# Hybrid attention and linear-attention layer on one core: values and gates loaded behind queries and keys, first sums of the last rows loaded early, first half of the out-projection spread over 20 steps more

## The chip, the cores and the metric

One core of a Trainium2 chip runs the kernel. The metric is the device time of one execution in microseconds. Three timed runs of the kernel before gave 996.18, 999.50 and 999.75 us (median 999.50); the profiled execution took 1000.02 us.

## The reference, cut to what matters

```python
h = rms_norm(x, pre_g)                       # x: 1024 rows of 1024
z = h @ w_in                                 # all projections at once
qa, ka, va, ga, qb, kb, vb, gb, gk_low = split_columns(z)
...
for each of 8 heads, 2 maps m, causal:       # differential attention, head size 2 x 64
    p[m] = softmax(mask(q[m] @ k[m].T * 64**-0.5))
    oa = (p[0] - lam * p[1]) @ v             # v: 1024 x 128
oa = rms_norm(oa, subln_g) * 0.8 * silu(ga)
...
ob = rms_norm(gla_chunked(qb, kb, vb, log_a), gla_g) * silu(gb)   # 4 heads, linear attention
y = concat([oa, ob]) @ w_out                 # 2048 -> 1024
return x + rms_norm(y, post_g)
```

All operands are float32. The kernel splits each operand of a product into a high and a low part (`hi`, `lo`) and forms the product from three matmuls (hi by hi, lo by hi, hi by lo).

## The kernel before, in words

**Three stages.** Until about 634 us the core computes the projections (accumulators `x`, `y`, `z` in the rows of the profile) and, woven in, the linear attention. Their results go to DRAM: queries and keys per head (`qk_d`), values (`v_d`), gates (`g_d`), and the linear attention's mixed output (`mixe`). Then follows the attention with the out-projection, and last the finishing of the eight blocks of 128 output rows.

**The attention stage is woven from three streams** by `merge`. Each stream is a generator that yields the cost of what it has just issued; a stream has a begin and an end on a common scale of steps and a total cost, and the one that is furthest behind issues next. The streams are:

- `all_scores`: head after head, row blocks qb from 7 down to 0. PE forms the scores (`sc`, first from `k`, then from `ks`, the other split of the keys), DVE takes the row maximum with the mask (L1037), ACT the exponential (L1047), POOL and DVE combine the two maps (L1053, L1056). After block 4 of a head the next head's queries and keys are loaded by `load_qk` (L877, L880) as far as their memory allows.
- `all_values`: PE turns the probabilities (`wtr`), ACT and DVE split them (`wt_hi`, `wt_lo`), PE multiplies by the values (`po`). Each head has a half 1 (rows 512 to 1023) that comes first and a half 0. `load_v` (L988) loads the next head's values after half 1; `attn_norm` loads the gate (L1118), forms the mean square with a matmul of ones (`ms`), applies norm and gate on POOL (L1140) and stores the result to DRAM (`mixd`, L1141). Of head 7 the result stays in memory as `last_mix`.
- `out_early`: the out-projection, as far as its inputs exist. First the linear attention's eight slices for all row blocks `st` (384 matmuls, `ypart`), then the slices of heads 0 to 3 (192 more `ypart`, stored from tile `yst` by a POOL DMA that adds to DRAM, L1304). These sums, `yd`, are read back at the end (tile `yp`) and copied by ACT into PSUM (`seed`, L1365), where PE adds the slices of heads 4 to 7 (`yps`). For the first blocks in the order `ENDS` = 4, 5, 6, 7, 0, 1, 2, 3, this begins inside the stage: slices of heads 4 to 6 are reloaded from `mixd` by `mix_pair` (tile `m_raw`, L1210), and slice 7 comes from `last_mix` (`last_part`, L1229).

**What sets the order.** PE's matmuls run in the order in which the source writes them; the other engines' and the DMA queue's order is chosen by a scheduler while the program is built. `tc.issue_after(ins)` puts what is issued inside it behind `ins` on the same queue; it is an order and no wait for the transfer. All loads and most stores go through the queue of SP, which issues one after the other: an instruction whose memory is not free yet holds all behind it.

**Memory.** Pools `kp` and `sm` hold tiles by tag. `kp` has one buffer each of 4 KB per partition for `q0`, `q1`, `k0`, `k1`, `ks0`, `ks1`. Odd heads put the first half of their keys (`k0`, `ks0`) into `sm` instead, so that `kp`'s `k0` and `ks0` are read for the last time by head 6, and `q0` by head 7. `yst` has two buffers of 2 KB; before the change both the sums that go out (`yst`) and the sums that come back within the stage (`yp`, L1312, L1323, L1338) share them.

Of the kernel before, what the change touches and what calls it, by code (L numbers as in the profile page):

```python
# [8 lines left out]
F32 = mybir.dt.float32  # L9
# [5 lines left out]
P = 128  # L15
# [16 lines left out]
def hymba_kernel(  # L32
# [58 lines left out]
    v_d = [tc.dram_tile([2, P, NT, P], F32, name=f"v{h}_d") for h in range(DA_HEADS)]  # L91
    g_d = [tc.dram_tile([P, S], F32, name=f"g{h}_d") for h in range(DA_HEADS)]
# [7 lines left out]
    yd = [[tc.dram_tile([P, 512], F32, name=f"y{st}{dh}_d") for dh in range(2)] for st in range(NT)]  # L100
# [3 lines left out]
    def bank(i, shape, name):  # L104
        return psum.tile(shape, F32, tag=f"b{i}", name=name)
# [47 lines left out]
    kp = ctx.enter_context(tc.tile_pool(name="kp", bufs=1))  # L153
# [63 lines left out]
    i = order.index((1, 4))  # L217
# [650 lines left out]
    def load_qk(h, n, half):  # L868

        if h % 2 and half == 0 and n != "q":  # L870
            t = smps[0].tile([P, 2, 512], F32R, tag=f"{n}0", name=f"{n}0")
        else:
            t = kp.tile([P, 2, 512], F32R, tag=f"{n}{half}", name=f"{n}{half}")
        for m in range(2):
            d = qk_d["q" if n == "q" else "k"][h][m, :, :, cols(half)]
            if n != "ks":
                sp.dma_start(fp(t[:, m]), d.rearrange("t p s -> (t p) s"))  # L877
            else:
                for i in range(2):
                    sp.dma_start(fp(t[64 * i : 64 * i + 64, m]), d[1 - i])  # L880
        qk[h, n, half] = t

    qk, smps = {}, []


    go(order.index((12, 5)) - made[0])
# [61 lines left out]
    SC, TR, PO, Y = order_b[:3], order_b[3:5], order_b[5], order_b[6:]  # L948
# [22 lines left out]
    smp = smp_cm.__enter__()  # L971
# [13 lines left out]
    def load_v(h):  # L985
        v = [smp.tile([P, NT, P], F32R, tag="v", name=f"v{t}", bufs=4) for t in range(2)]
        for t in range(2):
            ins = sp.dma_start(fp(v[t]), v_d[h][t])  # L988
            if h == 0:
                tc.keep_in_program_order(ins)  # L990
        return v
# [121 lines left out]
    def attn_norm(h, half, o):  # L1113
        if h < DA_HEADS - 1:
            gate = smp.tile([P, 512], F32, tag="gate", name="gate", bufs=2)
        else:
            gate = kp.tile([P, 512], F32, tag=("q1", "k1")[half], name="gate")
        sp.dma_start(gate, g_d[h][:, cols(half)])  # L1118
        sq = smp.tile([P, 512], F32, tag="r", name="sq", bufs=1)
        act.activation(sq, o, AF.Square)  # L1120
        hl = smp.tile([P, 2, 512], F32R, tag="sq_hl", name="sq_hl", bufs=1)
        act.copy(hl[:, 0], sq)
        dve.tensor_tensor(hl[:, 1], sq, fp(hl[:, 0]), ALU.subtract)
        if h == DA_HEADS - 1:

            dve.scalar_tensor_tensor(gate, o, sub_g, gate, ALU.mult, ALU.mult)
        yield 0.0
        yield 0.0
        n_tr[0] += 1
        ms = bank(TR[n_tr[0] % 2], [P, 512], "ms")  # L1130
        for i in range(2):
            mm(ms, ones, hl[:, i], start=(i == 0), stop=(i == 1))
        if h == DA_HEADS - 1 and not half:
            opened[TR[n_tr[0] % 2]] = None
        r = smp.tile([P, 512], F32, tag="r", name="r", bufs=1)
        act.activation(r, ms, AF.Ln, bias=eps_t, scale=1.0 / P)
        act.activation(r, r, AF.Exp, scale=-0.5)
        if h < DA_HEADS - 1:
            dve.scalar_tensor_tensor(r, o, sub_g, r, ALU.mult, ALU.mult)
            pool.tensor_tensor(gate, r, gate, ALU.mult)  # L1140
            sp.dma_start(mixd[h * P : (h + 1) * P, cols(half)], gate)  # L1141
            stored.append(h)
        else:
            dve.tensor_tensor(gate, gate, r, ALU.mult)
            last_mix[half] = gate
        yield 0.0
# [102 lines left out]
    def out_early():  # L1249

        part = mix0
        ps = [y_bank(0, dh, "ypart") for dh in range(2)]
        for e in range(E, E + 8):
            yield 1.0
            if e == E:
                nxt = mix(1)
            for dh in range(2):
                times(ps[dh], part, E, dh, e, E + 7)
            yield 1.0
        for dh in range(2):  # L1260
            sp.dma_start(yd[0][dh], y_tile(ps[dh]))
        for st in range(1, NT - 1):
            part, nxt = nxt, mix(st + 1)
            rows = slice(ENDS[st - 1] * P, ENDS[st - 1] * P + P)
            sp.dma_start(out[0, rows, :], x[0, rows, :])
            for dh in range(2):
                ps = y_bank(st, dh, "ypart")
                for e in range(E, E + 8):
                    times(ps, part, E, dh, e, E + 7)
                    yield 0.69  # L1270
                sp.dma_start(yd[st][dh], y_tile(ps))

# [12 lines left out]
        for dh in range(2):  # L1285
            kept = sp.dma_start(yd[NT - 1][dh], y_tile(ps[dh]))
        for n, st in enumerate(ENDS):
            part = nxt
            if n == 1:
                yield lambda: len(stored) >= 8  # L1290
            if n + 3 < NT:
                raws_o.append(load_mix(ENDS[n + 3], 0, 4))

            if 1 <= n <= 4:
                with tc.issue_after(kept.ins), tc.issue_after(mix_load[0]):
                    weights(3 + n)
            if n + 1 < NT:
                nxt = mix_part(ENDS[n + 1], 0, 4, raws_o.pop(0))
            for dh in range(2):
                ps = y_bank(st, dh, "ypart")  # L1300
                for e in range(4):
                    times(ps, part, 0, dh, e, 3)
                    yield 0.69
                pool.dma_start(yd[st][dh], y_tile(ps), accum_op=ALU.add)  # L1304
        yield lambda: len(stored) >= 2 * (DA_HEADS - 1) - 1
        mix_pair(0)
        for n, st in enumerate(ENDS[:2]):
            if n:
                yield lambda: scored
            for dh in range(2):  # L1310
                yp = smp.tile([P, 512], F32, tag="yst", name="yp", bufs=2)
                sp.dma_start(yp, yd[st][dh])  # L1312
                seed(st, dh, (Y, SC)[n][dh], yp)
            yield 0.7
        for st in ENDS[:2]:
            for dh in range(2):
                for e in range(4, 7):
                    last_times(st, dh, parts_d[st], e)
                    yield 0.69
            if st == ENDS[0]:  # L1320
                mix_pair(2)
                yp = smp.tile([P, 512], F32, tag="yst", name="yp", bufs=2)
                sp.dma_start(yp, yd[ENDS[2]][0])  # L1323
                seed(ENDS[2], 0, SC[2], yp)

    def mix_pair(n):

# [6 lines left out]

    def early_ends():

        yp = smp.tile([P, 512], F32, tag="yst", name="yp", bufs=2)
        sp.dma_start(yp, yd[ENDS[2]][1])  # L1338
        for e in range(4, 7):
            last_times(ENDS[2], 0, parts_d[ENDS[2]], e)  # L1340
        for st in ENDS[:2]:
            last_part(st, parts_d[st])
            for dh in range(2):
                last_times(st, dh, parts_d[st], 7)
        seed(ENDS[2], 1, PO, yp)
        for st in ENDS[2:4]:
            last_part(st, parts_d[st])

# [5 lines left out]
    LAST, ENDS = 2, [4, 5, 6, 7, 0, 1, 2, 3]  # L1354
# [6 lines left out]
    def seed(st, dh, b, yp):  # L1361
        open_bank(b)
        ps = ps_d[st, dh] = opened.pop(b, None) or bank(b, [P, 512], "yps")
        opened[b] = None
        pin(b not in Y, act.copy(ps, yp))  # L1365

    def last_times(st, dh, part, e):
# [8 lines left out]
    T = 8 * 36.0  # L1376
    LAG = 34.0
# [4 lines left out]
    merge(  # L1382
        [0.0, T, DA_HEADS * s_cost, all_scores()],
        [LAG, T + LAG, DA_HEADS * 10.0, all_values()],
        [-6.0, T + LAG, 16.0 + 14 * 5.52 + 16 * 2.76 + 11.8, out_early()],
    )


# [124 lines left out]
```

## Time and profile before

| | |
|---|---|
| median of three timed runs | 999.50 us |
| profiled execution | 1000.02 us, of which the span from the first to the last instruction 998.3 us |
| busy: PE, DVE, ACT, POOL | 966.6, 728.3, 591.6, 133.1 us |
| granted PE clock, mean | 0.995 |
| chain that ended last | PE 83%, DMA 8%, DVE 3%, ACT 3% |
| DMA queue of SP | 212.10 MB, 65.9% of the engines' span |

In a row of the time line the columns are the start in us from the span's start, the duration, engine, line, operation, what is written and read, and how often it repeats; in square brackets is how long the engine stood idle before it and what ended that. PE's matmuls overlap, so the distance from one start to the next is what one costs. In a row of a table by windows stand the window, its length, each engine's busy time with the number of instructions, the granted PE clock as a share of full speed, the busy share of the DMA engines and GB/s.

### The profile page before, as it was taken

To read this page: it belongs to the slowest core of one execution; us is meant where nothing else is said; L and a number is where in the kernel's file an instruction comes from. 1 tells how busy PE (TensorE), PEld (TensorE's weight loads), DVE (VectorE), ACT (ScalarE), POOL (GpSimd) and SP (SyncE) were. 2 spreads that over 40 slices of the span, in tenths; PEclk is the share of its full clock that TensorE was granted. 3 is DMA by queue.
4 is the path that set the end of the run, shared out by engine and by line. 5 is a ranking of instruction groups with operands and counts; after the bars stand their busy time and mean duration, and the time that the engine had idled before them with its cause. 6 is when DMAs were issued, how large, how long until landed. Compare 5 with 4: busy or idle time off the path is not lost.

```text
span 998.3 us, 15795 instructions
## 1 busy us (share of the span) xinstructions
PE 966.6 (97%) x5354; PEld 835.4 (84%) x5354; DVE 728.3 (73%) x1436; ACT 591.6 (59%) x1148; POOL 133.1 (13%) x143
## 2 busy tenths in 40 slices
PE   6999999999999999999999999989999999999896
PEld 5998988888889998998888888768888888888775
DVE  6986697789757487568778684667777788787455
ACT  7642464586466446345457674356676677687573
POOL 5200000000000001000000000011322233443122
PEclk9999999999999999999999999999999999999899
DMA  9443366747766678877987768895675679984567
GB/s 356 129 120 101 111 166 211 235 153 228 262 219 193 216 232 274 263 244 239 294 248 259 246 190 302 272 369 152 212 231 170 212 267 299 336 214 97 158 190 158
DMA packets 152593, 220.45 MB, mean 221 GB/s; under 512 B 17104, under 2 KB 83664, under 8 KB 152416
## 3 DMA queue, kind: packets, MB, share of 16 engines
q1 hardware_dynamic: 148480, 212.10, 65.9%
q0 software_dynamic: 4032, 7.34, 4.6%
q8 instruction: 42, 0.69, 0.3%
q14 instruction: 39, 0.32, 0.1%
HBM read 133.93 MB, written 88.60 MB: 223 GB/s over the span
## 4 chain that ended last, share of the span: by engine, by line
PE 83%; DMA 8%; DVE 3%; ACT 3%; SPq 1%; issue 1%; POOL 0%; DVEq 0%; ACTq 0%; POOLq 0%
PE x L117 20%; PE z L117 13%; PE y L117 13%; PE ypart L117 12%; PE sc L117 6%; PE po L117 5%; PE yps L117 4%; PE wtr L120 3%; PE gpo L117 2%; DMA wo_d<-wo_raw 2%; DMA wo_raw<-in_w_out_dram 1%; PE kv L117 1%; DMA v_d<-c 1%; PE gkl_ps L117 1%; DMA m_lo<-mixe 1%
## 5 line engine op out<-in xcount | busy, mean ns | idle before, releaser
L315 ACT CAST w<-w_raw 128x512 fp32r<-128x512 f32 (+1 forms) x164 | 112.5, 688 | 98.3 <-PE y L117 46.6
L316 DVE TENSOR_TENSOR w<-w_raw,w 128x512 fp32r<-128x512 f32 (+1 forms) x164 | 126.7, 774 | 48.9 <-ACT w L315 43.1
L1047 ACT ACTIVATE p<-p,stt 128x896 f32<-128x896 f32 (+7 forms) x128 | 99.4, 777 | 48.8 <-DVE stt L1037 48.1
L427 ACT COPY s<-x 128x512 f32<-128x512 f32 x84 | 49.0, 583 | 89.5 <-PE x L117 89.3
L1037 DVE CUSTOM_DVE_ANT_0 p<-sc,maskt 128x512 f32<-128x512 f32 (+3 forms) x128 | 74.7, 586 | 31.2 <-PE sc L117 30.1
L1053 POOL TENSOR_SCALAR p<-p,stt,lam 128x1024 f32<-128x1024 f32 (+3 forms) x64 | 54.7, 855 | 261.0 <-DVE stt L1052 252.1
L296 DVE TENSOR_TENSOR w_raw<-w_raw 128x512 f32<-128x512 f32 (+1 forms) x96 | 75.6, 787 | 17.0 <-DMA w_raw<-in_w_in_dram 15.6
L117 PE MATMUL z<-s_hi,w 128*128 128x512 f32 x320 | 80.2, 393 | 0.0
L117 PE MATMUL y<-h_hi,w 128*128 128x512 f32 x320 | 80.1, 392 | 0.0
L117 PE MATMUL x<-s_hi,w 128*128 128x512 f32 x320 | 80.0, 392 | 0.0
L117 PE MATMUL ypart<-wo_hi,m_hi 128*128 128x512 f32 x192 | 78.5, 409 | 0.1
L784 POOL TENSOR_SCALAR_AFFINE_SELECT gan<-gan 128x512 f32<-128x512 f32 x8 | 10.8, 1346 | 492.5 <-ACT gan L783 492.5
L117 PE MATMUL ypart<-wo_hi,m_lo 128*128 128x512 f32 x192 | 75.4, 393 | 0.0
L117 PE MATMUL ypart<-wo_lo,m_hi 128*128 128x512 f32 x192 | 75.4, 393 | 0.0
L117 PE MATMUL sc<-k,q 128*128 128x512 f32 (+1 forms) x192 | 70.3, 371 | 4.8 <-DMA q<-q_d 2.7
L117 PEld LDWEIGHTS x<-s_hi,w 128*128 128x128 f32 x320 | 59.4, 188 | 12.0
L117 PEld LDWEIGHTS y<-h_hi,w 128*128 128x128 f32 x320 | 59.3, 188 | 11.8
L117 PEld LDWEIGHTS z<-s_hi,w 128*128 128x128 f32 x320 | 59.1, 188 | 11.7
L117 PE MATMUL sc<-ks,q 128*128 128x512 f32 (+1 forms) x192 | 66.4, 348 | 1.2 <-DMA ks<-k_d 1.2
L1096 DVE TENSOR_TENSOR wt_lo<-wtr,wt_hi 128x512 fp32r<-128x512 f32 (+1 forms) x80 | 50.5, 633 | 14.8 <-ACT wt_hi L1095 14.4
L1095 ACT CAST wt_hi<-wtr 128x512 fp32r<-128x512 f32 (+1 forms) x80 | 42.9, 538 | 27.7 <-PE wtr L120 27.4
L1056 DVE SCALAR_TENSOR_TENSOR p<-p,stt,p 128x1024 f32<-128x1024 f32 (+3 forms) x64 | 53.1, 829 | 8.0 <-POOL p L1053 7.9
(224 smaller groups left out, 2242.3 us busy)
## 6 DMA issues: line engine op xcount, KB each, us to landing
w_raw<-in_w_in_dram SPq DMA_DIRECT2D x56, 512.0 KB, 4.7
wo_raw<-in_w_out_dram SPq DMA_DIRECT2D x32, 256.0 KB, 3.3
wo_d<-wo_hi SPq DMA_DIRECT2D x32, 256.0 KB, 3.3
wo_d<-wo_raw SPq DMA_DIRECT2D x32, 256.0 KB, 3.7
q<-q_d SPq DMA_DIRECT2D x32, 256.0 KB, 5.0
k<-k_d SPq DMA_DIRECT2D x32, 256.0 KB, 6.0
ks<-k_d SPq DMA_DIRECT2D x64, 128.0 KB, 6.0
wo_hi<-wo_d SPq DMA_DIRECT2D x16, 512.0 KB, 7.0
```

Source lines behind the costliest of these rows:

```text
L117: tc.keep_in_program_order(pe.matmul(*a, **k))
L120: tc.keep_in_program_order(pe.transpose(dst, src, ident))
L296: dve.tensor_tensor(dst, a, b, ALU.subtract)
L315: act.copy(w[0], src)
L316: dve.tensor_tensor(w[1], src, fp(w[0]), ALU.subtract)
L427: act.copy(b[k], ps)
L1037: ins = dve.tensor_tensor_reduce(p[:, a:e], sc[:, : e - a], maskt[:, NZ + P - (e - a) :] if last else maskt[:, : e - a], 1.0, 3e38 if i == ...
L1047: act.activation(p[:, :n], p[:, :n], AF.Exp, bias=st[:, m : m + 1], scale=-1.0, accum_out=st[:, 2 + m : 3 + m],)
L1053: pool.tensor_scalar(p1[:, :n], p1[:, :n], st[:, 5:6], lam, ALU.mult, ALU.mult)
L1056: dve.scalar_tensor_tensor(p0[:, :n], p0[:, :n], st[:, 4:5], p1[:, :n], ALU.mult, ALU.subtract)
L1095: act.copy(hi[:, :n], pt[:, :n])
L1096: dve.tensor_tensor(lo[:, :n], pt[:, :n], fp(hi[:, :n]), ALU.subtract)
```

## The change

Three edits. (1) `load_qk` notes its last DMA in `qk_load`; the values of heads 1 to 7 and all gates are put behind that DMA on SP's queue. (2) The six loads of first sums within the stage (`yp` for blocks 4, 5 and 6, two halves each) no longer use the two `yst` buffers; a function `sums_of` loads both halves of a block at once into `kp`'s `k0`, `ks0` and `q0`. (3) The end of `out_early`'s stretch moves from T + LAG = 322 to 342 steps, so that its matmuls stand later against the two other streams.

```diff
@@ load_qk
             if n != "ks":
-                sp.dma_start(fp(t[:, m]), d.rearrange("t p s -> (t p) s"))
+                ins = sp.dma_start(fp(t[:, m]), d.rearrange("t p s -> (t p) s"))
             else:
                 for i in range(2):
-                    sp.dma_start(fp(t[64 * i : 64 * i + 64, m]), d[1 - i])
+                    ins = sp.dma_start(fp(t[64 * i : 64 * i + 64, m]), d[1 - i])
+        qk_load[:] = [ins.ins]
@@ load_v
-            ins = sp.dma_start(fp(v[t]), v_d[h][t])
+            with tc.issue_after(qk_load[0]) if h else nullcontext():
+                ins = sp.dma_start(fp(v[t]), v_d[h][t])
@@ attn_norm
-        sp.dma_start(gate, g_d[h][:, cols(half)])
+        with tc.issue_after(qk_load[0]):
+            sp.dma_start(gate, g_d[h][:, cols(half)])
@@ out_early
-                yp = smp.tile([P, 512], F32, tag="yst", name="yp", bufs=2)
-                sp.dma_start(yp, yd[st][dh])
-                seed(st, dh, (Y, SC)[n][dh], yp)
+                seed(st, dh, (Y, SC)[n][dh], sums_of(n)[:, dh])
...
+    def sums_of(n):
+        if n not in sums_so_far:
+            yp = sums_so_far[n] = kp.tile([P, 2, 512], F32, tag=("k0", "ks0", "q0")[n], name="yp")
+            for dh in range(2):
+                sp.dma_start(yp[:, dh], yd[ENDS[n]][dh])
+        return sums_so_far[n]
@@ merge
-        [-6.0, T + LAG, 16.0 + 14 * 5.52 + 16 * 2.76 + 11.8, out_early()],
+        [-6.0, T + LAG + 20, 16.0 + 14 * 5.52 + 16 * 2.76 + 11.8, out_early()],
```

**SP's queue at the start of the attention stage.** A piece of the difference: `k_6680` and `ks_6683` are the first half of head 1's keys, `k_6672`, `q_6669` and `ks_6675` head 1's second half, `v_7050` and `v_7051` its values, and the two gates are head 0's.

```order
 L877 DMA k_6680<-k_d 128x512 x2
 L880 DMA ks_6683<-k_d 64x512 x4
-L988 DMA v_7050<-v_d 128x1024
-L988 DMA v_7051<-v_d 128x1024
-L1118 DMA gate<-g_d 128x512 x2
 L877 DMA k_6672<-k_d 128x512
 L877 DMA q_6669<-q_d 128x512 x2
 L877 DMA k_6672<-k_d 128x512
 L880 DMA ks_6675<-k_d 64x512 x4
```

Four DMAs of together 1.5 MB (two of values, two of gates) no longer stand ahead of the second half of head 1's queries and keys. In the changed kernel they stand further down the same queue, the values here as `v_7041` and `v_7042`, and one of the two gates; `q_6797` is head 1's first half of the queries, `k_7059` and `ks_7062` are head 2's keys:

```order
L880 DMA ks_6675<-k_d 64x512 x4
L1265 DMA y_d<-yst 128x512 x2
L928 DMA m_hi<-mixe 128x1024
L928 DMA m_lo<-mixe 128x1024
L877 DMA k_7059<-k_d 128x512
L877 DMA q_6797<-q_d 128x512 x2
L991 DMA v_7041<-v_d 128x1024
L991 DMA v_7042<-v_d 128x1024
L877 DMA k_7059<-k_d 128x512
L880 DMA ks_7062<-k_d 64x512 x4
L1122 DMA gate<-g_d 128x512
```

The values moved nine rows down, behind loads that need head 0's scores to be done; the second gate went further down still, behind the first store of `mixd`.

**PE where the final sums begin.** Before, around the first `yps` (`p_9701` and its neighbours are probabilities of head 7):

```order
L117 MATMUL po<-wt_lo,v_9748 128x512
L120 MATMUL wtr<-ident,p_9701 128x128
L120 MATMUL wtr<-ident,p_9648 128x128
L120 MATMUL wtr<-ident,p_9563 128x128
L120 MATMUL wtr<-ident,p_9478 128x128
L117 MATMUL yps<-wo_hi,m_hi 128x512
L117 MATMUL yps<-wo_hi,m_lo 128x512
L117 MATMUL yps<-wo_lo,m_hi 128x512
L117 MATMUL po<-wt_hi,v_9748 128x512
```

And in the changed kernel, around its first `yps`:

```order
L117 MATMUL po<-wt_lo,v_9706 128x512
L120 MATMUL wtr<-ident,p_9756 128x128
L120 MATMUL wtr<-ident,p_9722 128x128 x2
L117 MATMUL ms<-sq_hl,ones 128x512 x2
L117 MATMUL po<-wt_hi,v_9706 128x384
L117 MATMUL po<-wt_hi,v_9707 128x384
L117 MATMUL po<-wt_lo,v_9706 128x384
L117 MATMUL yps<-wo_hi,m_hi 128x512
L117 MATMUL yps<-wo_hi,m_lo 128x512
L117 MATMUL yps<-wo_lo,m_hi 128x512
```

The first `yps` moved behind the mean square of head 7's half 1. Counted over the whole order, 41 matmuls stand between the last score and the first `yps` before (18 `ypart`, 9 `po`, 12 `wtr`, 2 `ms`), and 113 now (51, 30, 28, 4); 58 of the 194 `yps` stand ahead of the last `ms` before, and 43 now. Between the first and the last score stand 552 `ypart` before and 519 now; between the first score and the first of head 1, 57 and 51. The number of matmuls as a whole is the same.

**SP's queue at the end of the stage.** Before:

```order
L1141 DMA mixd<-gate 128x512
L1118 DMA gate<-g_d 128x512 x3
L1141 DMA mixd<-gate 128x512
L1210 DMA m_raw<-mixd 128x3x128 x4
L1312 DMA yp<-y_d 128x512 x2
L1141 DMA mixd<-gate 128x512
L1312 DMA yp<-y_d 128x512 x2
L1323 DMA yp<-y_d 128x512
L1338 DMA yp<-y_d 128x512
```

And now:

```order
L1334 DMA yp<-y_d 128x512 x3
L1122 DMA gate<-g_d 128x512
L1145 DMA mixd<-gate 128x512
L1122 DMA gate<-g_d 128x512 x3
L1145 DMA mixd<-gate 128x512
L1334 DMA yp<-y_d 128x512 x2
L1214 DMA m_raw<-mixd 128x3x128 x4
L1145 DMA mixd<-gate 128x512
```

All six loads of first sums moved ahead of the four loads of `m_raw`. The first of them stands six rows above the first row shown, directly ahead of the load of head 7's `q0`; the last two (block 6, in the memory of `q0`) stand between the store of head 6's half 1 and the loads of `m_raw` that read it.

More of the change, by code (lines that the diff above doesn't have):

```diff
@@ L876, in load_qk @@
             if n != "ks":
-                sp.dma_start(fp(t[:, m]), d.rearrange("t p s -> (t p) s"))
+                ins = sp.dma_start(fp(t[:, m]), d.rearrange("t p s -> (t p) s"))
             else:
                 for i in range(2):
-                    sp.dma_start(fp(t[64 * i : 64 * i + 64, m]), d[1 - i])
+                    ins = sp.dma_start(fp(t[64 * i : 64 * i + 64, m]), d[1 - i])
+        qk_load[:] = [ins.ins]
         qk[h, n, half] = t
-    qk, smps = {}, []
+    qk, smps, qk_load = {}, [], []
     go(order.index((12, 5)) - made[0])
@@ L1321, in out_early @@
                 mix_pair(2)
-                yp = smp.tile([P, 512], F32, tag="yst", name="yp", bufs=2)
-                sp.dma_start(yp, yd[ENDS[2]][0])
-                seed(ENDS[2], 0, SC[2], yp)
+                seed(ENDS[2], 0, SC[2], sums_of(2)[:, 0])
+    sums_so_far = {}
+    def sums_of(n):
[4 more added lines that the diff above has]
+        return sums_so_far[n]
     def mix_pair(n):
@@ L1335, in early_ends @@
     def early_ends():
-        yp = smp.tile([P, 512], F32, tag="yst", name="yp", bufs=2)
-        sp.dma_start(yp, yd[ENDS[2]][1])
         for e in range(4, 7):
@@ L1344, in early_ends @@
                 last_times(st, dh, parts_d[st], 7)
-        seed(ENDS[2], 1, PO, yp)
+        seed(ENDS[2], 1, PO, sums_of(2)[:, 1])
         for st in ENDS[2:4]:
```

## The prediction

> **What bounds the kernel now.** I read the page's first line, then a table by windows of the last third, then PE's time line where the table shows PE idle, and last the time lines of the engines that PE waited for.
>
> ```profile
> PE 966.6 (97%) x5354; PEld 835.4 (84%) x5354; DVE 728.3 (73%) x1436; ACT 591.6 (59%) x1148; POOL 133.1 (13%) x143
> ```
>
> PE is busy 97% of the span, and its matmuls stay the same in number and size. What the change can bring is therefore only what PE loses in idle time or at a lower clock, in the stage that is edited.
>
> ```profile
> 640.00:660.00 20.00, 17.90 (x83) 14.02 (x82) 15.57 (x49) 11.87 (x28) 5.36 (x6) 1.00 0.88 273
> 660.00:680.00 20.00, 16.08 (x83) 13.14 (x82) 11.59 (x32) 9.32 (x21) 2.41 (x4) 1.00 0.85 302
> ...
> 680.00:920.00 240.00, 240.00 (x1276) 204.24 (x1275) 188.15 (x517) 171.09 (x375) 75.52 (x79) 1.00 0.73 224
> ...
> 920.00:940.00 20.00, 16.83 (x74) 13.69 (x73) 11.80 (x25) 11.42 (x27) 5.86 (x7) 0.83 0.67 147
> ```
>
> From 680 to 920 PE never idles. It loses 2.1 us in 640 to 660, 3.9 in 660 to 680, and in 920 to 940 it loses 3.2 and also runs at a clock of 0.83. These three places and the last 40 us are all there is to win.
>
> **The first place: head 1's queries and keys come late.**
>
> ```profile
> 648.51 0.38 PE L117 MATMUL sc<-k,q 128*128 128x256 f32 x1 [1.23 <-DVE stt L1037]
> ...
> 664.66 0.47 PE L117 MATMUL sc<-k,q 128*128 128x512 f32 x1 [2.74 <-DMA q<-q_d]
> ...
> 667.89 0.47 PE L117 MATMUL sc<-ks,q 128*128 128x512 f32 x1 [1.17 <-DMA ks<-k_d]
> ```
>
> The 2.1 us are waits of scores for DVE (the first row is the longest). The 3.9 us are the last two rows: 2.74 for head 1's queries, 1.17 for its keys. What stood ahead of them in SP's queue:
>
> ```profile
> 654.93 1.58 SPq L988 DMA_DIRECT2D v<-v_d  x2
> 656.78 1.28 SPq L1118 DMA_DIRECT2D gate<-g_d  x2
> 658.28 0.32 SPq L877 DMA_DIRECT2D k<-k_d  x1
> 658.79 0.79 SPq L877 DMA_DIRECT2D q<-q_d  x2
> ...
> 660.86 2.94 SPq L880 DMA_DIRECT2D ks<-k_d  x4
> ```
> ```profile
> v<-v_d SPq DMA_DIRECT2D x4, 512.0 KB, 5.3
> gate<-g_d SPq DMA_DIRECT2D x2, 256.0 KB, 5.7
> ```
> ```profile
> 658.00:661.00 3.00, 3.00 (x21) 2.63 (x20) 2.64 (x12) 2.16 (x7) 1.20 (x2) 1.00 1.04 365
> 661.00:664.00 3.00, 0.92 (x7) 0.54 (x5) 1.42 (x8) 1.49 (x6) 1.00 (x2) 1.00 1.04 402
> ```
>
> Two values of 512 KB and two gates of 256 KB, 1.57 million bytes, went out first, and the DMA engines were full (share 1.04) at 365 to 402 GB/s. Taking them out frees 1.57 MB / 385 GB/s = 4.1 us of transfer, and on SP the 658.28 − 654.93 = 3.4 us that they took to issue. So the queries land about 4.1 us earlier, ready near 660.5 in place of 664.6, the last keys near 663.6 in place of 667.7. PE wants them earlier too: 51 `ypart` in place of 57 stand ahead of head 1's first score, 6 × 0.23 = 1.4 us (pitch below), so it arrives at 661.9 − 1.4 = 660.5 and needs those keys some 1.9 us later, at 662.4. The queries are just in time; the keys are 1.2 us late. **Gain 3.9 − 1.2 = 2.7 us.** Ends: 3.9 if both come in time, 0 if DVE is what PE waits for next. What is pushed back is not late: head 1's values are read after all 36 `po` of head 0, 39 us of PE work behind head 0's last score.
>
> The 2.1 us of waits for DVE stay as they are: the scores of head 0 come about as dense (24 score matmuls by the same point of PE's work in both orders). Ends −2.1 and +2, value 0.
>
> **The second place: the first final sums start late, and cold.**
>
> ```profile
> 917.60 0.62 PE L117 MATMUL ms<-sq_hl,ones 128*128 128x512 f32 x2
> ...
> 922.53 0.40 PE L117 MATMUL sc<-ks,q 128*128 128x512 f32 x1
> ...
> 930.31 0.60 PE L120 MATMUL wtr<-ident,p 128*128 128x128 f32 x4
> 934.08 0.80 PE L117 MATMUL yps<-wo_hi,m_hi 128*128 128x512 f32 x1 [3.17 <-ACT yps L1365]
> ...
> 939.15 0.63 PE L117 MATMUL yps<-wo_hi,m_lo 128*128 128x512 f32 x1
> 939.58 0.63 PE L117 MATMUL yps<-wo_lo,m_hi 128*128 128x512 f32 x1
> ...
> 940.51 0.39 PE L117 MATMUL po<-wt_lo,v 128*128 128x512 f32 x1
> 940.74 0.40 PE L117 MATMUL yps<-wo_hi,m_hi 128*128 128x512 f32 x1
> 940.98 0.39 PE L117 MATMUL yps<-wo_hi,m_lo 128*128 128x512 f32 x1
> ```
> ```profile
> 936.00:938.00 2.00, 2.00 (x6) 1.51 (x5) 0.28 (x1) 0.00 (x0) 0.00 (x0) 0.50 0.68 241
> 940.00:942.00 2.00, 2.00 (x10) 1.65 (x9) 0.03 (x1) 1.15 (x2) 0.00 (x0) 0.97 0.33 112
> ```
>
> PE idles 3.17 us, and behind the gap the granted clock is 0.50: matmuls of 512 columns start 0.43 us apart (939.15 to 939.58), from 940.5 on 0.23 to 0.24 apart. In 934.08 to 940.51 stand 14 matmuls of 512 columns and three turns of 128 (0.11 each at full clock), 14 × 0.23 + 0.33 = 3.55 us of work in 6.43 us: 2.88 lost. The place costs 3.17 + 2.88 = 6.05 us.
>
> The Trainium skill (TensorE: Matmul & The Clock Gate, What's actually happening) has the clock halve after an idle window of about 3.4 us and come back after about 3.4 us of work. The trace halves it after 3.17, not after the 2.74 at 664.66, and keeps it low for 6 us, not 3.4; by the page's 3.4 us the loss would be 1.7 in place of 2.88 and the sum below 1.2 us smaller. The measured stretch decides.
>
> What PE waited for:
>
> ```profile
> 929.96 4.42 SPq L1312 DMA_DIRECT2D yp<-y_d  x2
> ```
> ```profile
> 923.23 0.32 SPq L1141 DMA_DIRECT2D mixd<-gate  x1
> 925.25 2.12 SPq L1210 DMA_DIRECT2D m_raw<-mixd  x4
> ```
> ```profile
> 930.22 0.51 ACT L1331 CAST m_hi<-m_raw 128x384 fp32r<-128x384 f32 x1 [1.11 <-DMA m_raw<-mixd]
> ...
> 933.41 0.61 ACT L1365 COPY yps<-yp 128x512 f32<-128x512 f32 x1
> 938.09 0.59 ACT L1365 COPY yps<-yp 128x512 f32<-128x512 f32 x1 [4.07 <-DMA yp<-y_d]
> ```
>
> Two chains end here. One is the first sum: its two loads issue from 929.96 to 934.38, since each needs a `yst` buffer, and the copy to PSUM comes at 933.41 and 938.09. The other is head 6's half 1, from its mean square at 917.60 over the store at 923.23 and the reload at 925.25 to ACT at 930.22, 12.6 us. Edit 2 ends the first chain: the memory of `k0` and `ks0` is free when head 6's scores end, a whole head earlier, and what waits behind these loads on SP (head 7's `q0`) needs the same scores to end. The last two loads, in the memory of `q0`, wait for head 7's last score; that ends at 922.9, ahead of the store at 923.23, so they do not hold the reload back. Alone, edit 2 would not help much, since the second chain sets 930.2. Edit 3 covers that: between the same mean square and the first `yps` the changed order has 57 `ypart`, 39 `po`, 32 `wtr`, 8 scores and 6 of ones; the 57 alone are 57 × 0.23 = 13.1 us, with the rest about 26.7, against 13.1 before. The chain of 12.6 us, lengthened by two issues of sums ahead of `m_raw` (L1312 took about 0.4 each), ends some 13 us early. The copy into the bank of the last `ypart` is not late either: its `yps` come 4.7 us of PE work behind it, and ACT needs two copies of 0.6. **Gain 6.05 us.** Ends: 3.17 less if a gap opens elsewhere and chills the clock again, nothing gained if both do.
>
> What is late next is the mean square of head 7's half 1: it stands 2.7 us of PE work behind its last `po`, and its feed on ACT takes longer:
>
> ```profile
> 946.38 0.59 ACT L1185 COPY o<-po 128x512 f32<-128x512 f32 x1 [0.76 <-PE po L117]
> ...
> 947.95 0.62 ACT L1122 CAST sq_hl<-sq 128x512 fp32r<-128x512 f32 x1
> ```
>
> 946.38 to 948.57 is 2.2, and DVE's half of the split about 0.7 more with a few tenths between: 3.1. **Cost 0.4 us** (0 to 1).
>
> **The third place: the last slice.**
>
> ```profile
> 954.70 0.50 PE L117 MATMUL yps<-wo_hi,m_hi 128*128 128x512 f32 x1 [0.26 <-ACT m_hi L1229]
> 955.43 0.50 PE L117 MATMUL yps<-wo_hi,m_lo 128*128 128x512 f32 x1 [0.23 <-DVE m_lo L1230]
> ...
> 959.37 0.50 PE L117 MATMUL yps<-wo_hi,m_hi 128*128 128x512 f32 x1 [0.22 <-ACT m_hi L1229]
> ...
> 990.13 0.39 PE L117 MATMUL yps<-wo_lo,m_hi 128*128 128x512 f32 x1
> ```
>
> Three short waits, 0.7 us, for the split of head 7's result. 15 `yps` more stand behind the last `ms` now (151 for 136), 15 × 0.23 = 3.4 us of cover, so they go: **gain 0.7** (0 to 0.7). Behind the last matmul 998.3 − 990.4 = 7.9 us of finishing stay.
>
> **Edit 3 between the ends** takes 33 of 552 `ypart` from between the scores, 33 × 0.23 = 7.6 us of 240: DVE goes from 188.15 / 240 = 78% to 188 / 232 = 81%, ACT from 71 to 74%. I cost it at 0, since PE had no idle time there at all; the cover that could go is the DVE time between scores, and that is the third rival.
>
> **Sum**, on the profiled execution: 1000.02 − 2.7 − 6.05 − 0.7 + 0.4 = 990.97. The median of the timed runs stands 0.5 below the profiled execution, so 990.5.
>
> **The rivals.**
>
> (1) The start's wait is only handed on: with the DMA engines full until 670 or DVE late, PE still loses 3 to 4 us before 668, and only the end is gained: 1000.02 − 6.05 − 0.3 = 993.7, or 993.2 by the median. For it: DVE is 78% busy there and PE already waits for it. Against it: the waits at 664.66 and 667.89 name DMAs alone.
>
> (2) The end's gap opens again a little further on: ACT, whose order is in sequence, holds the first copies or the split behind a turn of probabilities, PE idles 3 us near the first `yps` and runs cold again: 1000.02 − 2.7 − 0.7 = 996.6, or 996.1. For it: two copies, four splits and the mean square's feed fall into the same 8 us. Against it: ACT is 11.42 of 20 us busy there.
>
> (3) Slower: denser scores make PE wait for DVE. In 640 to 660, with DVE 78% busy, PE lost 2.1 of 20 us. At that rate over the 232 us between, it would lose 24 us: 991 + 24 = 1015. It decides from 4% lost, 9.05 of 232 us; at 6.5% it is slower by 0.5% and more. Against it: at the same 78% from 680 to 920 PE lost nothing.
>
> (4) The edits meet no end of a wait and all stays within 0.5%, 995 to 1004: for instance (1) and (2) together, 999.7.
>
> **How the numbers follow.** Forecast (both gaps gone, 987.5 to 993) 0.70; rival (1) 0.13; (2) 0.07; (4) 0.06; (3) 0.04. The range takes in the ends: low, all of the start (3.9 and 2.1) and no cost at `ms`, 999.5 − 3.9 − 2.1 − 6.05 − 0.7 = 986.8; high, rival (1) with another 2 us of waits for DVE, 995.2. It leaves out (2), (3) and (4). A measurement of this kernel tells about 0.5% from no change, here under 994.5: forecast and most of (1), 0.82; within, the rest of (1), (2) and (4), 0.14; slower 0.04.
>
> **What would show it.** In the changed profile PE's first score of head 1 should wait under 0.5 us and the second under 2, and the window of 20 us around the first `yps` should be 20.00 busy at a clock of 1.00. PE should stay at full busy time between. Wrong would be: waits of `sc` for DVE of over 2 us in the middle, an idle time of 3 us with clock 0.50 anywhere behind the last score, or a `ypart` that waits for SP's loads of weights.

## The result, and the profile after

The changed kernel takes **988.24 us** (median of 6 runs, 987.03 to 990.33), the kernel before on the same chip 998.45 (6 runs, 996.18 to 999.85): ratio 0.9902, 95% interval 0.9884 to 0.992. By the ratio that is 9.8 us less (8.0 to 11.6). 990.5 us was forecast. The profiled execution of the changed kernel took 990.33 us with a span of 988.6.

PE's work is the same 5354 instructions, in a span that is 9.7 us shorter:

```profile
PE 964.7 (98%) x5354; PEld 834.9 (84%) x5354; DVE 728.5 (74%) x1436; ACT 590.7 (60%) x1148; POOL 138.3 (14%) x143
```

The table by windows (us, then busy time and instructions of PE, PEld, DVE, ACT, POOL, then granted clock, DMA share, GB/s) at the places that the prediction spoke of:

```profile
640.00:660.00 20.00, 18.76 (x88) 15.21 (x87) 15.66 (x50) 11.56 (x23) 4.15 (x4) 1.00 0.92 298
660.00:680.00 20.00, 19.88 (x104) 16.35 (x102) 15.29 (x44) 11.69 (x28) 4.72 (x6) 1.00 0.86 303
680.00:920.00 240.00, 239.92 (x1282) 204.14 (x1281) 192.61 (x528) 174.84 (x386) 77.74 (x79) 1.00 0.74 232
920.00:940.00 20.00, 19.30 (x100) 15.91 (x100) 10.70 (x16) 13.16 (x26) 7.57 (x6) 1.00 0.68 125
```

PE was 17.90, 16.08, 240.00 and 16.83 busy in these before. All that PE still waits for from 630 us on stands in two rows (total, times, longest, in us):

```profile
PE sc L117 <- DVE stt L1040: 1.2, 2, 1.0
PE po L117 <- DVE wt_lo L1099: 0.7, 1, 0.7
```

Before, the same view added up to 9.9 us: 3.2 for the first final sum, 2.7 and 1.2 for head 1's queries and keys, 2.1 for DVE, 0.7 in the last slice. On PE's time line, the first two scores of head 1, and the place of the first final sums:

```profile
662.26 0.50 PE L117 MATMUL sc<-k,q 128*128 128x512 f32 x1
...
664.50 0.47 PE L117 MATMUL sc<-ks,q 128*128 128x512 f32 x1
...
934.05 0.96 PE L117 MATMUL ms<-sq_hl,ones 128*128 128x512 f32 x2
...
935.39 0.40 PE L117 MATMUL yps<-wo_hi,m_hi 128*128 128x512 f32 x1
935.63 0.40 PE L117 MATMUL yps<-wo_hi,m_lo 128*128 128x512 f32 x1
...
937.87 0.39 PE L117 MATMUL po<-wt_lo,v 128*128 128x256 f32 x1 [0.70 <-DVE wt_lo L1099]
```

No score of head 1 waits for a load. The first `yps` waits for nothing, and the next starts 0.24 us behind it, the pitch of full clock. The one gap left here is new, so the window from 920 to 940 is 19.30 us busy and not 20.00 as forecast. DVE's time line names what PE waits for:

```profile
934.66 2.69 DVE L1343 TENSOR_TENSOR m_lo<-m_raw,m_hi 128x384 fp32r<-128x384 f32 x2 [0.21 <-ACT m_hi L1342]
937.27 0.54 DVE L1099 TENSOR_TENSOR wt_lo<-wtr,wt_hi 128x384 fp32r<-128x384 f32 x1
```

The splits of the reloaded results now fall into the last turns of head 7, and two of them (2.69 us) stand in DVE's sequence ahead of the `wt_lo` that PE needs.

SP's queue shows why the loads are in time:

```profile
655.66 0.33 SPq L877 DMA_DIRECT2D k<-k_d  x1
656.88 1.09 SPq L877 DMA_DIRECT2D q<-q_d  x2
...
659.15 2.37 SPq L880 DMA_DIRECT2D ks<-k_d  x4
...
665.65 0.91 SPq L991 DMA_DIRECT2D v<-v_d  x2
...
913.67 0.32 SPq L1145 DMA_DIRECT2D mixd<-gate  x1
914.10 0.87 SPq L1334 DMA_DIRECT2D yp<-y_d  x2
916.14 3.03 SPq L1214 DMA_DIRECT2D m_raw<-mixd  x4
```

The values issue behind the keys, and the four reloads of `m_raw` are issued by 919.2, 16 us ahead of the first `yps`; before, they were issued by 927.4, 6.7 ahead.

To compare the two executions without what happened earlier, take the stretch from the first `ypart` to the last matmul. Its last matmul starts at 990.13 before (shown above); its first, before and after, and its last after:

```profile
633.91 0.39 PE L117 MATMUL ypart<-wo_hi,m_hi 128*128 128x512 f32 x1
```
```profile
637.06 0.39 PE L117 MATMUL ypart<-wo_hi,m_hi 128*128 128x512 f32 x1
```
```profile
981.32 0.39 PE L117 MATMUL yps<-wo_lo,m_hi 128*128 128x512 f32 x1
```

The stage went from 356.2 to 344.3 us: **12.0 us less**. The span shows only 9.7 less because the changed execution reached the stage 3.15 us later, in code that was not changed, and finished 0.9 faster behind the last matmul. 1.7 of the 3.15 are one stretch of half clock at 465.6, told below.

### The profile page after: what moved, and what is told of

It is laid out like the page before. It is cut to its first block, busy times and chain, and to the rows that moved or that the text cites. A ratio compares the mean times of both kernels' runs of the same rounds, so it can differ in the third digit from the quotient of the medians.

```text
span 988.6 us, 15784 instructions
## 1 busy us (share of the span) xinstructions
PE 964.7 (98%) x5354; PEld 834.9 (84%) x5354; DVE 728.5 (74%) x1436; ACT 590.7 (60%) x1148; POOL 138.3 (14%) x143
## 4 chain that ended last, share of the span: by engine, by line
PE 85%; DMA 6%; DVE 4%; ACT 3%; issue 2%; SPq 1%; POOL 0%; DVEq 0%; ACTq 0%; POOLq 0%
PE x L117 20%; PE z L117 14%; PE y L117 13%; PE ypart L117 13%; PE sc L117 7%; PE po L117 5%; PE yps L117 4%; PE wtr L120 3%; PE gpo L117 2%; DMA wo_d<-wo_raw 1%; DMA wo_raw<-in_w_out_dram 1%; PE kv L117 1%; DMA v_d<-c 1%; PE gkl_ps L117 1%; PE ms L117 1%
## 5 line engine op out<-in xcount | busy, mean ns | idle before, releaser
L784 POOL TENSOR_SCALAR_AFFINE_SELECT gan<-gan 128x512 f32<-128x512 f32 x8 | 14.0, 1744 | 494.4 <-ACT gan L783 494.4
```

## The experiments

The three edits keep their numbers: 1 for the order of the loads, 2 for the memory of the first sums, 3 for the 20 steps. The kernel before took 999.7, 998.5 and 1000.58 us (medians) in the three sets of runs made for these experiments, so kernels are compared by ratio. The code below is cut to the lines that matter.

**One edit at a time.** Edit 1 alone (in part: `load_qk` also notes its last DMA, and the load of the gates has the same wrapper):

```
-            ins = sp.dma_start(fp(v[t]), v_d[h][t])
+            with tc.issue_after(qk_load[0]) if h else nullcontext():
+                ins = sp.dma_start(fp(v[t]), v_d[h][t])
```

> Edit 1 alone (values and gates behind queries and keys). As predicted: PE's waits for head 1's queries and keys (2.74 and 1.17 us) shrink to 0 to 1.2 us, the gap at the first final sums and its clock of 0.50 stay as before, so 2.7 to 3.9 us faster than before. Rival (the wait is only handed on to DVE or to full DMA engines): PE still loses 3 us or more before 668 us, time within 1 us of before.

Measured: 998.01 us (12 runs), ratio 0.9976 (0.9957 to 0.9995), 2.4 us less. No score waits for a load any more, the three waits for DVE are as before (0.59, 0.27, 1.23), and the end keeps its gap; one row of the waits carries that:

```profile
PE yps L117 <- ACT yps L1368: 3.3, 1, 3.3
```

Edit 1 does what it says, and 2.7 us had been put on it.

Edit 2 alone (in part: the other two places that load a first sum change in the same way, and `sums_of` is added):

```
-                yp = smp.tile([P, 512], F32, tag="yst", name="yp", bufs=2)
-                sp.dma_start(yp, yd[st][dh])
-                seed(st, dh, (Y, SC)[n][dh], yp)
+                seed(st, dh, (Y, SC)[n][dh], sums_of(n)[:, dh])
```

> Edit 2 alone (first sums into the memory of dead keys). The prediction said that alone it would not help much, since the reload of head 6's half 1 ends at 930.2: gap shrinks by under 1 us, the clock still halves, 0 to 2 us faster. Rival: the first reload, which is all that the first final matmul needs, is on ACT at 928.0 already, only the second at 930.2; then the gap closes and the clock stays, 5 to 6 us faster, and edit 3 is not needed for it.

Measured: 998.29 us (12 runs), ratio 0.9993 (0.9973 to 1.0014): no change that can be told. PE's time line at the first final sums:

```profile
930.98 0.50 PE L117 MATMUL yps<-wo_hi,m_hi 128*128 128x512 f32 x1 [0.91 <-ACT m_hi L1337]
...
933.29 0.74 PE L117 MATMUL po<-wt_hi,v 128*128 128x512 f32 x2 [0.99 <-ACT wt_hi L1095]
...
934.92 0.50 PE L117 MATMUL po<-wt_lo,v 128*128 128x512 f32 x1 [0.89 <-DVE wt_lo L1096]
```

The wait for the copy of the first sum is gone, and PE waits 0.91 for `m_hi`, the split of the reloaded result, and then 0.99 and 0.89 for a turn that the copies and splits delay. This is the second chain of the prediction. The start differs too, though its code and its order of loads are those of before: PE waits 0.40 us for head 1's queries and 1.01 for its keys, in place of 2.74 and 1.17, and a stretch of half clock at 648.6 stands ahead of them (1.71 us by the granted clock). PE comes to head 1 1.1 us later (29.1 us behind the first `ypart`, 28.0 before), and SP issues its queries 1.2 us earlier (23.7 and 24.9 behind it). So the 3.9 us at the start are the measure of one execution.

Edit 3 alone:

```
-        [-6.0, T + LAG, 16.0 + 14 * 5.52 + 16 * 2.76 + 11.8, out_early()],
+        [-6.0, T + LAG + 20, 16.0 + 14 * 5.52 + 16 * 2.76 + 11.8, out_early()],
```

> Edit 3 alone (stretch of the early out-projection 20 steps longer). As predicted: the first sums still wait for the two yst buffers until the last store of a ypart sum has gone out, so a gap of 3 us or more with clock 0.50 stands at the first final matmul, now behind the mean square of head 7: within 1.5 us of before. Rival (cover is all that was missing): 113 matmuls behind the last score hide the loads, 5 to 6 us faster.

Measured: 997.94 us (12 runs), ratio 0.9984 (0.9962 to 1.0006), not told from no change. Two places of PE's time line say where its gain goes:

```profile
663.68 0.76 PE L117 MATMUL sc<-k,q 128*128 128x512 f32 x1 [4.74 <-DMA q<-q_d]
...
940.56 0.50 PE L117 MATMUL yps<-wo_hi,m_hi 128*128 128x512 f32 x1 [1.47 <-ACT yps L1365]
...
944.34 0.50 PE L117 MATMUL yps<-wo_hi,m_hi 128*128 128x512 f32 x1 [0.76 <-ACT yps L1365]
...
949.14 0.50 PE L117 MATMUL yps<-wo_hi,m_hi 128*128 128x512 f32 x1 [1.79 <-ACT yps L1365]
```

With fewer partial sums ahead of it PE comes to head 1 earlier and waits 4.74 us for the queries (2.74 before); and with the sums still in the two `yst` buffers the one gap at the end becomes three, 4.0 us together.

The last kernel of this set is the kernel before with 12 extra matmuls in an unused bank ahead of the first `yps`; they change no output. It keeps PE busy in the gap, to measure the clock's part alone:

```
+        warm = bank(SC[2], [P, 512], "warm")
+        for i in range(12):
+            mm(warm, ones, wo[4][0][:, :512], start=(i == 0), stop=(i == 11))
```

> The kernel before with 12 matmuls of ones by a weight tile, written to a free PSUM bank that nobody reads, ahead of the first final matmul. They fill 12 x 0.23 = 2.8 us of the 3.2 us gap. If the half clock comes from PE's idle time, the matmuls behind the gap start 0.23 us apart in place of 0.43 and 2 to 2.9 us are gained. If the slow pitch comes from something else, nothing is gained (0 to 1 us slower).

Measured: 1000.11 us (12 runs), ratio 1.0002 (0.9987 to 1.0017). In the profile the gap is filled, and the granted clock is 1.00 in all windows from 920 to 960:

```profile
933.41 0.50 PE L117 MATMUL yps<-wo_hi,m_hi 128*128 128x512 f32 x1 [0.49 <-ACT yps L1368]
```

So it is the idle PE that brings the half clock on here. But the time did not fall with it: a gain over 1.3 us is excluded by the interval, and 2.9 had been worked out from one profile. That the clock itself improved shows over all executions: (1 - granted clock) x span is 4.9 us on average over the 12 executions, 7.0 for the kernel before in the same set. The traces show a part of why the time does not follow. From the first `yps` to the last matmul, the same 194 `yps` with the rest of the work, it is 56.05 us in the kernel before (990.13 - 934.08) and 54.62 here (988.03 - 933.41): 1.4 us less, not 2.9. At full clock PE comes to the next copies and splits sooner and is held there: the second first sum is copied by ACT from 937.24 to 937.83, and its first matmul starts at 937.88. By this the half clock had in part covered these waits. Where the rest of the gain went is not shown.

**Two edits of the three** (the same lines as above, one edit left out each time), and the whole change with 40 steps:

```
-        [-6.0, T + LAG + 20, 16.0 + 14 * 5.52 + 16 * 2.76 + 11.8, out_early()],
+        [-6.0, T + LAG + 40, 16.0 + 14 * 5.52 + 16 * 2.76 + 11.8, out_early()],
```

> Edits 1 and 2 without 3. If edit 3 is what covers the reload of head 6's half 1, the gap at the first final sums stays as in edit 2 alone (waits of 0.9, 1.0 and 0.9 us and a half clock), and only the start's wait goes: 3 to 4.5 us faster than before. Rival (edits 1 and 2 are enough): 8 us and more faster.

> Edits 2 and 3 without 1. The end's gap is closed as in the full change, but fewer early matmuls stand ahead of head 1's first score, so that PE waits there for the queries as in edit 3 alone (4.7 us, with a stretch at a lower clock): 3 to 6 us faster than before. Rival (edit 1 adds nothing beside 2 and 3): 9 us and more faster.

> Edits 1 and 3 without 2. The start is as in the full change; at the end the first sums still need the two yst buffers, so that PE waits some 4 us in three places for their copies, as in edit 3 alone: 5.5 to 7.5 us faster than before, 2.5 to 4 slower than the full change. Rival (the memory of the sums does not matter once the matmuls are spread): as fast as the full change, 9 to 10.5.

> The full change with 40 steps in place of 20. All early matmuls are then done before the first final one, which stands 4.9 us of PE work behind the last product with the values. If what is left at the end (0.7 us for the split of probabilities and 0.3 for the mean square) comes from ACT's copies of first sums between them, it goes, and the time is 0 to 1.5 us under that of the full change, 10 to 11.5 under before. Rival (scores that stand another 3% denser make PE wait for DVE): PE waits of over 2 us for DVE between 660 and 900, 0 to 4 us slower than the full change.

| kernel | us (runs) | ratio (95%) | less than before, us |
|---|---|---|---|
| 1 and 2 | 996.61 (11) | 0.9986 (0.9974 to 0.9998) | 1.4 |
| 2 and 3 | 995.65 (11) | 0.9965 (0.9953 to 0.9977) | 3.5 |
| 1 and 3 | 993.51 (6) | 0.9947 (0.993 to 0.9964) | 5.3 |
| 1, 2 and 3 | 988.24 (6) | 0.9902 (0.9884 to 0.992) | 9.8 |
| 1, 2 and 40 steps | 993.05 (6) | 0.9948 (0.9929 to 0.9968) | 5.2 |

One row from each of the first three kernels, in this order, with what PE waits for when an edit is missing:

```profile
931.36 0.50 PE L117 MATMUL yps<-wo_hi,m_hi 128*128 128x512 f32 x1 [1.29 <-ACT m_hi L1340]
```
```profile
663.88 0.77 PE L117 MATMUL sc<-k,q 128*128 128x512 f32 x1 [4.59 <-DMA q<-q_d]
```
```profile
937.38 0.56 PE L117 MATMUL yps<-wo_hi,m_hi 128*128 128x512 f32 x1 [1.83 <-ACT yps L1368]
```

Edits 1 and 2 gave less than the 3 to 4.5 us expected of them, and edits 1 and 3 a little less than 5.5 to 7.5. Each missing edit brings back the wait that it covers for the others: without 3 the reload, without 1 the queries, without 2 the buffers of the first sums. Alone the edits gave 2.4, 0.7 and 1.6 us, 4.7 in all; together they gave 9.8.

With 40 steps the scores at the start become too dense for DVE:

```profile
650.54 0.50 PE L117 MATMUL sc<-k,q 128*128 128x512 f32 x1 [2.22 <-DVE stt L1039]
```

There are 2.9 us of waits for DVE in that profile, 1.2 at 20 steps; from 680 to 920 PE is still 239.97 of 240 busy. So the prediction's third rival shows here, at the start only, when edit 3 is taken further. The size was missed by the expectation (0 to 1.5 us faster than the changed kernel) and by its rival (0 to 4 slower): by the ratios the kernel is 4.6 us slower. The waits for DVE make 1.7 of it, and a wait for the copy of a final sum another 0.9; the rest is not traced to a cause.

**How sharp the choice of 20 is, and whether the rest can be had.** 10 and 30 steps (the same number), then two edits on the changed kernel at a wait that neither the change nor the prediction touched: at 464 us, in the earlier stage, PE waits for the split ahead of a mean square.

> The whole change, with 10 steps more in place of 20. With 0 steps (edits 1 and 2 alone) 996.6 us, with 20 988.2, with 40 993.05. Theory (20 is broad enough a choice: each 10 steps move about 16 partial sums, 3.8 us of PE work, behind the last scores; the reload of head 6's half 1 is late by 1.3 us with 0 steps, so 3.8 us are enough to cover it): PE idles less than 0.5 us near the first final sum, the start loses 1 to 2 us to DVE as with 0 and 20, and the time is 988 to 990, ratio 0.989 to 0.992. Rival (20 is a narrow optimum, or the 0-step gap needs more cover because the waits for the split of the weights, 0.99 and 0.89, stay): 992 to 995, with a half clock between 930 and 945.

> The whole change, with 30 steps. Theory (denser scores at the start make PE wait for DVE and the half clock follows by chance: DVE waits of 1.25 us at 20 steps, 3 at 40): DVE waits of 1.5 to 3 us between 640 and 662, the end as at 20, and 990 to 992 us, ratio 0.991 to 0.994, between the two. Rival (the loss at 40 comes from the end alone, the 0.9 us at the copy of a final sum): 988 to 989 us with DVE waits under 1.3.

10 steps: 990.99 us (6 runs), ratio 0.9903 (0.9887 to 0.992). 30 steps: 990.26 us (6 runs), ratio 0.9901 (0.9883 to 0.9919). Both equal 20 (0.9902). The profile at 10 steps has no wait at the first final sums, so 10 steps cover the reload already (in its place PE waits 1.37 us at 852.55 for a split of probabilities, in the stretch where the kernel before and the changed one never wait); at 30 steps the waits have grown to 1.6 for DVE, 1.1 for a key and 1.2 at a final sum, and the ratio does not show it. The waits for DVE came as the theory had them, its price of 2 us or more over 20 steps did not, though the interval does not exclude it. The plateau is broad: 0 steps 0.9986, 10 to 30 steps 0.990, 40 steps 0.9948.

The first edit at 464 us fills the wait with matmuls of ones:

```
+            for i in range(20 if (g, half) == (2, 0) else 0):
+                mm(ms[:, :P], ones, ones, start=(i == 0), stop=(i == 19))
             for i in range(2):
                 mm(ms, ones, hl[:, i], start=(i == 0), stop=(i == 1))
```

> The changed kernel with 20 matmuls of 128x128 of ones (about 0.11 us each, 2.2 us in all) put ahead of the mean square of the earlier stage at 464 us, where PE idles 1.87 and 0.48 us and the profile of the changed kernel shows a clock of 0.83 behind it. They write the bank that the mean square then overwrites, so they change no output. Theory (idle PE at this one place halves the clock by chance and makes up much of the 2 us per execution that the changed kernel still loses to the clock): idle there falls to about 0.6, the mean clock goes from 0.998 to 0.999, the time falls by 0 to 1.5 us, 987 to 988.2. Rival (the clock goes down for another reason, wherever PE's load falls): mean clock 0.998 and time as the changed kernel's within 0.5 us. Below what the comparison tells, 0.2%, the mean clock of the executions decides.

The second takes it away, by a step more between the split and the mean square:

```
             yield
             yield
             yield
+            if (g, half) == (2, 0):
+                yield
             ms, ib = take_bank([P, 512], "gms")
```

> The changed kernel with one more step between the split and the mean square at 464 us, so that 24 matmuls of 256 columns (3 us of PE work) stand between them. It takes the wait away instead of filling it. Theory: PE's idle time of 2.35 us at that place goes, and what the clock loses behind it; 988.2 - 2.35 - 0 to 1.5 = 984.4 to 985.9 us, ratio to before 0.986 to 0.988. Rival: the later steps of the same stage each come a step later and open another wait (for a bank, or for the reload of the next gates), and the time is 987 to 990.

Filled: 991.79 us (6 runs), ratio 0.9922 (0.9905 to 0.9939). Moved by a step: 991.21 us (6 runs), ratio 0.991 (0.989 to 0.993). Neither is better than the changed kernel (0.9902), and the mean granted clock, which was to decide on the filled one, is 0.997 over its six executions and 0.998 in the changed kernel: no gain. The gap at 464 went in both, and came back. In the filled kernel it stands at the next mean square, since ACT's split is queued behind a cast that waits for a load of weights (first row PE, second ACT):

```profile
502.29 1.69 PE L117 MATMUL gms<-sq_hl,ones 128*128 128x512 f32 x2 [2.57 <-ACT sq_hl L836]
```
```profile
500.58 0.62 ACT L584 CAST wo_hi<-wo_raw 128x512 fp32r<-128x512 f32 x1 [5.22 <-DMA wo_raw<-in_w_out_dram]
```

In the moved one, 2.2 us of waits stand at 514 and 540 in place of 2.35 at 464. In this stage the wait that both took from PE reappeared further on within 80 us, once behind a load. In the late stage, where PE is busy from 680 to 920 before and after, what the three edits took away together did not come back.

## Why the prediction was right

Its mechanism held at all three places, and its sum for the profiled execution, 990.97, was met by 990.33. That the two are so close is partly luck: the stage that was edited gained 12.0 us where 9.05 had been summed, and the changed execution lost 3.15 of them ahead of the stage, 1.7 by a stretch of half clock in code that was not changed. The parts, in us of the profiled executions:

| step of the prediction | predicted | measured |
|---|---|---|
| head 1's queries and keys | -2.7 | -3.9 |
| waits of scores for DVE | 0 | -0.8 |
| gap ahead of the first `yps` | -3.17 | -3.2 |
| half clock behind it (6.83 us at half clock, of which PE idles 0.79) | -2.88 | -3.0 |
| short waits of the last slice | -0.7 | -0.7 |
| new waits at head 7's mean square and turn | +0.4 | +0.3 and +0.7 |
| not assigned, in the stage | | -1.4 |
| ahead of the stage and behind it | 0 | +3.15 and -0.9 |
| sum | -9.05 | -9.7 |

- **The start** was put too low. The keys were to be 1.2 us late, and in this profile they are in time. SP issues the first of the keys in question (head 1's second half) 18.6 us behind the first `ypart` (655.66 - 637.06); before it was 24.4 (658.28 - 633.91). That is 5.8 us earlier where 3.4 had been taken. In edit 1 alone it is 20.8, 3.6 earlier and so about as taken; 18.5 to 19.7 stand only in the kernels that have edit 3 too. What edit 3 adds here was not in the sum, and why it does is not shown. How near the edge this is shows in the other kernels with edit 1: the wait for the keys was 0 in five of them (the changed one, edit 1, edits 1 and 2, 10 and 40 steps), 0.2 and 0.8 in two, and 1.05 and 1.06 in two.
- **"The 2.1 us of waits for DVE stay"** was a term of 0 that came to -0.8: with 20 steps the longest wait is 0.96, with none 1.23. It does not go one way: at 0, 10, 20, 30 and 40 steps the waits are 2.1, 1.3, 1.2, 1.6 and 2.9 us. Both ends had been in the range.
- **The end** went as worked out, and the two chains were both there. From head 6's mean square (908.27 in the changed profile) to the first `yps` it is 27.1 us, where 26.7 had been worked out. "Alone, edit 2 would not help much", since the reload comes next: made alone it gave 0.7 us, which the interval does not tell from none, and the row at 930.98 names `m_hi`. "Edit 3 covers that": without it 1.4 us are gained, with it 9.8.
- **"ACT, in sequence, holds the first copies or the split"** (the second rival) came in a small form: 0.70 us at 937.87, on DVE in place of ACT. The prediction had put 0.4 on the mean square (0 to 1), where the second of its two matmuls now starts some 0.3 late (the row at 934.05), and nothing on the turn.
- **The parts do not add up edit by edit**, which the sum hid. It had the start and the end as two terms that each stand alone. Taken out of the whole change, edit 1 is worth 6.3 us (9.8 - 3.5), edit 2 4.5 and edit 3 8.4; alone they are worth 2.4, 0.7 and 1.6. The sum was right because all three are in.
- **The first rival** (the wait is only handed on at the start) did not come: 1.2 us in place of 6.0. **The fourth** is excluded by the interval.

What is not shown is how much of the 9.8 us is waits, and how much clock. Over all executions of the kernel before in a set, (1 - granted clock) x span is 6.1 to 7.3 us on average, in the changed kernel 2.0 over its 6, of which 0.8 to 2.9 (in the profiles of this study) lie behind the last matmul and cost nothing. By that at most some 4 to 5 of the 9.8 us are clock. But the kernel with 12 extra matmuls lost 2.1 us less to the clock than the kernel before and was not faster, within 1.3 us; so the split stays open.

## What to carry to other kernels

When a wait is to be taken away, list what else is ready only a little earlier, and change these together: three edits that gave 0.7 to 2.4 us alone gave 9.8 together. Test a change of several parts by leaving one out, not only by making one alone. And look for gaps in a stage where PE otherwise hardly waits; in the earlier stage here, the gap at 464 us came back further on when it was taken away.

## What the runs showed of the hardware

**The half clock comes in whole windows of a grid that runs on through the execution.** In 14 profiles there are 20 stretches of half clock ahead of the last matmul, and every one of them takes 1.70 to 1.71 us of PE's clock (14 of them) or 3.41 to 3.42 (6 of them), as (1 - granted clock) summed over windows of half a microsecond: they are 3.41 or 6.83 us long, never anything between. In edit 1 alone they begin at 463.61, 651.34 and 934.65: 187.73 us and 283.31 us apart, which is 55 and 83 times 3.4133. In edits 1 and 2 they begin at 463.23, 650.96 and 934.27, the same distances. So the grid stands still within an execution, and its place differs from one to the next. Laid on that grid, the kernel before around its first `yps` and around the first score of head 1 (same columns as above, the clock third from the end):

```profile
929.87:933.28 3.41, 1.04 (x7) 0.67 (x5) 2.39 (x3) 3.06 (x7) 1.25 (x2) 1.00 0.54 165
933.28:936.70 3.42, 2.62 (x6) 2.16 (x7) 3.00 (x4) 0.74 (x2) 0.91 (x1) 0.50 0.75 93
936.70:940.11 3.41, 3.41 (x11) 2.65 (x11) 0.56 (x1) 1.07 (x2) 0.00 (x0) 0.50 0.73 234
940.11:943.52 3.41, 3.41 (x19) 2.85 (x18) 0.35 (x1) 1.66 (x3) 0.00 (x0) 1.00 0.50 162
660.22:663.64 3.42, 1.70 (x12) 1.28 (x11) 2.17 (x9) 2.27 (x8) 1.00 (x2) 1.00 1.03 405
663.64:667.05 3.41, 2.05 (x10) 1.51 (x10) 1.56 (x4) 0.53 (x1) 0.00 (x0) 1.00 1.06 346
```

and the changed kernel around its one stretch, in code that both kernels share:

```profile
462.18:465.59 3.41, 1.15 (x5) 0.79 (x6) 3.29 (x6) 2.29 (x6) 0.00 (x0) 1.00 0.51 179
465.59:469.00 3.41, 3.41 (x18) 3.41 (x17) 3.12 (x5) 2.00 (x4) 0.00 (x0) 0.50 0.58 177
469.00:472.42 3.42, 3.42 (x20) 2.94 (x19) 3.09 (x5) 0.92 (x2) 0.00 (x0) 1.00 0.86 224
```

A window in which PE idles 2.37 or 2.26 us (3.41 - 1.04, 3.41 - 1.15) is followed by one at half clock. The wait of 2.74 us for head 1's queries falls across a border, 1.72 us of idle time in one window and 1.36 in the next, and the clock stays. Over all windows of the 14 profiles from 15 us on that ran at full clock themselves: idle for more than 1.83 us, 22 of 22 were followed by half clock; for 1.48 to 1.83, 5 of 13; for less, none of 3925. The limit is about half a window, as well as modelled ends of matmuls can tell. Why the stretch is one window long in 14 cases and two in 6 stays open: PE is idle 0.79 us in the half-clock window shown at 933.28, which a second one follows, and elsewhere 0.52 and 0.57 brought no second one, 0.28 and 0.49 did.

The prediction read the Trainium skill (TensorE: Matmul & The Clock Gate, What's actually happening) as giving 3.4 us for the time at half clock, against 6 us measured, and it took the length of the gap (3.17 against 2.74 us) for what decides. What decides is how the gap falls on the grid: a wait of 1.83 us at 937.38 (edits 1 and 3) brought the half clock, the one of 2.74 did not. The same section says that the window of 3413 ns runs free of the kernel; the 283.31 us / 83 = 3.4133 here agree to the last digit, and the 6 us are two windows. Where the section speaks of an idle window, 1.84 idle of 3.41 us were enough (edits 1 and 3, at 934).

So what a gap takes from the clock on top of itself is a matter of chance: 0, 1.7 or 3.4 us. The 3.28 us gap in edit 1 alone lay in two windows (1.47 and 1.99 us idle) and took 1.7; the 3.17 of before took 3.4, less 0.4 for the time in which PE stood idle anyway; the 2.74 for the queries took nothing, and 2.22 with 40 steps took 1.7. The time can lose less than that, where PE would have had to wait at full clock: from the first `yps` to the last matmul it is 56.05 us with two windows (before), 55.32 with one (edit 1 alone, 988.37 - 933.05) and 54.62 with none (12 extra matmuls), with the same 194 `yps`: about 0.7 us for each window. That is why one profile misjudges the clock's part in either direction. Over executions the time goes with the clock: the correlation of the two is -0.82, -0.52 and -0.60 over the 35, 23 and 11 runs of the kernel before in the three sets, and -0.97 over 6 of the changed one.
